# The GELU of the state space outputs: one ScalarE function, or square, tanh and two fused VectorE products

## The chip, the cores and the metric

The kernel runs on one core of one Trainium2 chip. The metric is the device time of one execution in microseconds (us), the median of several runs. Each run is one launch of the whole program.

## The reference, cut to what matters

The reference is one layer of a streaming encoder over 2048 prompt frames and 32 sample frames. After a norm and one input projection, half of the columns go through banded attention (`q`, `k`, `v`), the other half (`u`, 32 groups of 16 channels) through a diagonal state space scan. The scan's outputs are passed through a tanh-form GELU and a sigmoid gate; both halves are normed, joined and projected; a gated feed-forward block follows.

```python
ssm_y, h_last = _s5(u, h0, ...)
g = jax.nn.gelu(ssm_y)
ssm_o = g * jax.nn.sigmoid(g @ lw['ssm_glu_w'] + lw['ssm_glu_b'])
merged = concatenate([_rmsnorm(attn, ...), _rmsnorm(ssm_o, ...)])
x = x + g1 * (merged @ lw['w_out'])
```

`jax.nn.gelu` is here 0.5 y (1 + tanh(sqrt(2/pi) (y + 0.044715 y^3))).

## The kernel before, in words

Products of f32 quality are made of three matmuls each (`mm3`, L119; the matmul itself is L117): both operands are split into a rounded part and a rest (`split`, L112: ScalarE copies, VectorE or GpSimd subtracts).

The program has three stages that overlap at their edges. In the first (to about 380 us) come the input norm and the projections. In the second (about 380 to 592 us) three flows run beside each other: the 32 state space groups (`ssm_group`, L950 on, flow `fm`), the projections of six late tiles (`deferred`, flow `fd`) and the attention tiles (`attention_tile`, flow `fa`). Towards its end, the weights of the gate and of the output projection are split as well (`glu_steps`, `wo_steps`). In the third stage, from about 590 us, the gate (`c_prep`), the output projection (`c_out`) and the last attention tiles run, and then the feed-forward block, which takes the longer part of the time.

One state space group: the inputs are transposed into the PSUM tile `up`; `uh` and `ul` are split from it; six matmuls give `v1` and `v2` in PSUM; VectorE multiplies them by tables into `w` and `t`; GpSimd adds; two VectorE scans run over `w`; VectorE or GpSimd multiplies by the tables again; seven matmuls sum up the PSUM tile `y` (128 x 262); ScalarE writes GELU(y) into `g2`, which is the buffer of `t` again (L992). In the next step the SP queue sends `g2` to DRAM (`gt_d`, L994) and GpSimd copies four columns of it (`gsm`, L995). The third stage reads `gt_d` and `gsm` back.

`y` has one PSUM buffer (`YB` is 1), so the matmuls of the next group wait until `y` has been read. The SBUF tiles of a group (`part`) have five buffers (`PSB`), and up to seven groups are under way (`Flow(ssm_start, G, 7, 1)`). The steps of the flows are emitted by fixed counts (`FM`, `FDS`, `FAS`); the order on each engine is then set when the program is built, by a scheduler that goes by this emission and a simulated timeline (`schedule_with_timeline_sim=True`). Each engine takes its instructions in that order.

ScalarE functions in use: copies and squares everywhere, `Exp` in `softmax` (L1057, L1059), `Tanh` for the gate (L1326) and once at the start (L223), the GELU function (L992), and `Silu` in the feed-forward block (L1741). The program names no tables; the build puts an ACT_TABLE_LOAD where the next function is not in the loaded set.

Helpers: `act` (L100, its instructions on L101) is every ScalarE operation, `stt` (L97, L98) VectorE's fused `(a op0 scalar) op1 b`, `tt` (L88, L89) every two-operand operation on VectorE or GpSimd.

Of the kernel before, what the change touches and what calls it, by code (L numbers as in the profile page):

```python
# [10 lines left out]
F32 = mybir.dt.float32  # L11
F32R = mybir.dt.float32r
I32 = mybir.dt.int32
AF = mybir.ActivationFunctionType
ALU = mybir.AluOpType
AX = mybir.AxisListType
MULT, ADD, SUB = ALU.mult, ALU.add, ALU.subtract
# [56 lines left out]
def hybrid_kernel(  # L74
# [13 lines left out]
    def tt(e, out, a, b, op):  # L88
        e.tensor_tensor(out, a, b, op=op)  # L89
# [7 lines left out]
    def stt(out, a, s, b, op0, op1):  # L97
        V.scalar_tensor_tensor(out, a, s, b, op0=op0, op1=op1)  # L98

    def act(out, a, func=AF.Copy, **kw):  # L100
        A.activation(out, a, func, **kw)  # L101

    def f(a):
        return a.bitcast(F32)
# [7 lines left out]
    def split(hi, lo, src, eh, el):  # L112
        cp(eh, hi, src)
        tt(el, lo, src, f(hi), SUB)

    def mm(out, lhsT, rhs, start, stop, more=False):
        PE.matmul(out, lhsT, rhs, start=start, stop=stop, skip_group_check=more)  # L117

    def mm3(out, ah, al, bh, bl, start, stop, more=False):  # L119

        mm(out, ah, bh, start, False, more)
        mm(out, ah, bl, False, stop and al is None, more)
        if al is not None:
            mm(out, al, bh, False, stop, more)
# [797 lines left out]
    def mbank(shape, dt=F32, nm="mb", tag="mb", bufs=MB):  # L922
        return bs1.tile(shape, dt, tag=tag, name=nm, bufs=bufs)
# [23 lines left out]
    def part(t, dt=F32R):  # L947
        return pss.tile([128, XC], dt, tag=t, name=t)

    def ssm_group(g):  # L950
        b_, gi_ = divmod(g, GB)
        us, uss = bt_[b_]
        sm = pss.tile([128, SM], F32R, tag="sm", name="sm", bufs=SMB)
        SP.dma_start(f(sm), sm_d[g])
        ec = pss.tile([128, 2, XC], F32, tag="ec", name="ec", bufs=SMB)
        for h in range(2):
            SP.dma_start(ec[64 * h:64 * h + 64], e_d[g])
        Th, Tl = sm[:, 0:128], sm[:, 128:256]
        M1, M2 = f(sm[:, 256:384]), f(sm[:, 384:512])
        up = mbank([128, XC], nm="up")  # L960
        yield 1
        for b in range(2):
            PE.transpose(up[:, 128 * b:128 * b + 128], us[:, b, gi_].rearrange("c l h -> c (l h)"), ident)
        PE.transpose(up[:, 256:262], uss[:, gi_].rearrange("c l h -> c (l h)"), ident[0:6, 0:6])
        uh, ul = part("uh"), part("ul")
        split(uh, ul, up, A, V)
        yield 1
        v1 = mbank([128, XC], nm="v1", tag="v1", bufs=1)
        v2 = mbank([128, XC], nm="v2", tag="v2", bufs=1)
        mm3(v1, sm[:, 512:640], sm[:, 704:832], uh, ul, True, True)  # L970
        mm3(v2, sm[:, 576:704], sm[:, 768:896], uh, ul, True, True)
        w = part("w", F32)
        t = part("t", F32)
        tt(V, w[:, 1:XC], v1[:, 0:XC - 1], ec[:, 0, 1:XC], MULT)
        tt(V, t[:, 1:XC], v2[:, 0:XC - 1], ec[:, 1, 1:XC], MULT)
        tt(P, w[:, 1:XC], w[:, 1:XC], t[:, 1:XC], ADD)
        P.tensor_copy(w[:, 0:258:257], zh[:, g])
        V.tensor_tensor_scan(w[:, 1:257], r8[:, g:g + 1].to_broadcast([128, 256]), w[:, 1:257], 0.0, op0=MULT, op1=ADD)
        V.tensor_tensor_scan(w[:, 258:262], r8[:, g:g + 1].to_broadcast([128, 4]), w[:, 258:262],
                             zh[:, g, 1:2], op0=MULT, op1=ADD)  # L980
        yield 1
        for i, (e, xf) in enumerate(((P, xf1), (P if g % 2 else V, xf2))):
            x = w if i else t
            tt(e, x, w, ec[:, i], MULT)
            P.tensor_copy(xf[:, :, g], x[:, 256:262:5])
        yield 1
        y = mbank([128, XC], nm="y", tag="y", bufs=YB)
        mm3(y, Th, Tl, uh, ul, True, False)
        mm(y, M1, t, False, False)
        mm(y, M2, w, False, True)  # L990
        g2 = t
        act(g2, y, AF.Gelu_apprx_tanh)  # L992
        yield 1
        SP.dma_start(gt_d[16 * g:16 * g + 16].rearrange("h l c -> l h c"), g2[:, 0:256])  # L994
        P.tensor_copy(gsm[:, :, g], g2[:, 257:261])  # L995
        yield 1
# [3 lines left out]
    def ssm_start(g):  # L1000
        if g % GB == 2 and g // GB < 3:
            ssm_batch(g // GB + 1)
        return ssm_group(g)
# [905 lines left out]
```

## Time and profile before

| | us |
|---|---|
| median of 3 runs | 2326.4 (2324.03 to 2329.42) |
| the profiled execution | 2332.55 |
| its span, first to last instruction | 2330.8 |
| TensorE busy, of the span | 2211.3 |
| VectorE busy | 1718.3 |
| ScalarE busy | 1261.2 |
| GpSimd busy | 1256.3 |

The rows of the trace come from the profiled execution, which took 6.15 us more than the median; 1.75 us of its time lie outside the span. PE is TensorE, PEld its weight loads, DVE VectorE, ACT ScalarE, POOL GpSimd, SP the queue that issues the DMAs. A granted clock of 1.00 is 2.4 GHz, of 0.50 it is 1.2 GHz; values between are a mixture over a stretch.

### The profile page before, as it was taken

To read this page: it belongs to the slowest core of one execution; us is meant where nothing else is said; L and a number is where in the kernel's file an instruction comes from. 1 tells how busy PE (TensorE), PEld (TensorE's weight loads), DVE (VectorE), ACT (ScalarE), POOL (GpSimd) and SP (SyncE) were. 2 spreads that over 40 slices of the span, in tenths; PEclk is the share of its full clock that TensorE was granted. 3 is DMA by queue.
4 is the path that set the end of the run, shared out by engine and by line. 5 is a ranking of instruction groups with operands and counts; after the bars stand their busy time and mean duration, and the time that the engine had idled before them with its cause. 6 is when DMAs were issued, how large, how long until landed. Compare 5 with 4: busy or idle time off the path is not lost.

```text
span 2330.8 us, 39040 instructions
## 1 busy us (share of the span) xinstructions
PE 2211.3 (95%) x13286; PEld 2055.1 (88%) x13286; DVE 1718.3 (74%) x2737; ACT 1261.2 (54%) x2544; POOL 1256.3 (54%) x1173
## 2 busy tenths in 40 slices
PE   7888898898899999999999998999999999999999
PEld 4576776786788888799999998999999989999998
DVE  6888874678777884766768779556677796677887
ACT  6655443555666655544445566444455754444664
POOL 1167775776366764578884136555521375565122
PEclk8899998898899999999999999999999999999999
DMA  7757676676323125457666644643365436534653
GB/s 232 264 169 239 192 219 205 196 232 200 102 75 93 55 69 174 150 174 219 209 200 213 184 142 154 180 122 111 101 199 170 132 110 183 147 97 120 199 164 125
DMA packets 429573, 380.12 MB, mean 163 GB/s; under 512 B 57327, under 2 KB 358987, under 8 KB 429373
## 3 DMA queue, kind: packets, MB, share of 16 engines
q1 hardware_dynamic: 429372, 377.63, 53.1%
q8 instruction: 104, 1.70, 0.3%
q14 instruction: 97, 0.79, 0.1%
HBM read 284.63 MB, written 92.91 MB: 162 GB/s over the span
## 4 chain that ended last, share of the span: by engine, by line
PE 63%; DVE 6%; ACT 2%; issue 2%; POOL 1%; DMA 1%; SPq 0%; DVEq 0%; POOLq 0%; ACTq 0%
PE fx L117 30%; PE fy L117 15%; PE fz L117 8%; PE co L117 5%; PE cb L117 1%; PE ob L117 1%; DVE wl L89 1%; PE pt L1070 1%; PE ft L1454 1%; ACT pbuf L101 1%; DVE ss L1332 1%; DVE bl L89 0%; PE fo L1721 0%; PE s L117 0%; DVE gl L89 0%
## 5 line engine op out<-in xcount | busy, mean ns | idle before, releaser
L89 DVE TENSOR_TENSOR wl<-wr,wh 128x512 fp32r<-128x512 f32 (+1 forms) x708 | 641.0, 921 | 252.2 <-ACT wh L101 248.9
L101 ACT ACTIVATE wh<-wr 128x512 fp32r<-128x512 f32 (+1 forms) x708 | 431.1, 617 | 552.7 <-PE fx L117 301.5
L117 PE MATMUL fx<-bh,wh 128*128 128x352 f32 (+1 forms) x1576 | 507.4, 322 | 6.2 <-DVE acc L98 3.8
L117 PE MATMUL fx<-bl,wh 128*128 128x352 f32 (+1 forms) x1576 | 506.4, 321 | 4.3 <-DVE bl L89 4.3
L117 PE MATMUL fx<-bh,wl 128*128 128x352 f32 (+1 forms) x1576 | 507.4, 322 | 0.0
L89 POOL TENSOR_TENSOR wr<-wr 128x512 f32<-128x512 f32 x256 | 388.0, 1525 | 185.6 <-DVE wl L89 138.9
L117 PEld LDWEIGHTS fx<-bh,wh 128*128 128x128 f32 x1576 | 298.1, 189 | 6.9 <-DVE acc L98 4.0
L117 PEld LDWEIGHTS fx<-bl,wh 128*128 128x128 f32 x1576 | 298.0, 189 | 5.2 <-DVE bl L89 5.2
L117 PEld LDWEIGHTS fx<-bh,wl 128*128 128x128 f32 x1576 | 297.6, 189 | 0.1
L89 POOL TENSOR_TENSOR c<-c,acc 128x352 f32<-128x352 f32 (+1 forms) x72 | 93.0, 1296 | 311.0 <-ACT c L101 293.2
L117 PE MATMUL fy<-bh,wh 128*128 128x352 f32 (+1 forms) x792 | 254.8, 322 | 1.1 <-DVE acc L98 0.8
L117 PE MATMUL fy<-bh,wl 128*128 128x352 f32 (+1 forms) x792 | 254.1, 321 | 0.0
L117 PE MATMUL fy<-bl,wh 128*128 128x352 f32 (+1 forms) x792 | 253.7, 320 | 0.0
L89 POOL TENSOR_TENSOR c<-c 128x352 f32<-128x352 f32 (+1 forms) x96 | 135.8, 1416 | 174.5 <-ACT wh L101 73.6
L117 PEld LDWEIGHTS fy<-bh,wh 128*128 128x128 f32 x792 | 149.6, 189 | 1.6 <-DVE acc L98 1.0
L117 PEld LDWEIGHTS fy<-bl,wh 128*128 128x128 f32 x792 | 149.4, 189 | 0.0
L117 PEld LDWEIGHTS fy<-bh,wl 128*128 128x128 f32 x792 | 149.0, 188 | 0.0
L89 DVE TENSOR_TENSOR bl<-q,bh 128x1408 fp32r<-128x1408 f32 (+3 forms) x85 | 140.7, 1660 | 5.1 <-ACT bh L101 5.1
L117 PE MATMUL fz<-bh,wl 128*128 128x352 f32 (+1 forms) x412 | 132.2, 324 | 4.5 <-DVE wl L89 4.5
L117 PE MATMUL fz<-bh,wh 128*128 128x352 f32 (+1 forms) x412 | 133.6, 325 | 1.0 <-ACT wh L101 0.9
L117 PE MATMUL fz<-bl,wh 128*128 128x352 f32 (+1 forms) x412 | 132.6, 322 | 0.0
L101 ACT ACTIVATE bh<-q 128x1408 fp32r<-128x1408 f32 (+3 forms) x85 | 108.5, 1284 | 17.4 <-DVE q L89 14.6
(388 smaller groups left out, 5135.3 us busy)
## 6 DMA issues: line engine op xcount, KB each, us to landing
wr<-in_w_gate_dram SPq DMA_DIRECT2D x132, 256.0 KB
wr<-in_w_up_dram SPq DMA_DIRECT2D x132, 256.0 KB
wr<-sd_d SPq DMA_DIRECT2D x96, 256.0 KB
wr<-in_w_down_dram SPq DMA_DIRECT2D x72, 256.0 KB
adw<-in_w_ada_dram SPq DMA_DIRECT2D x64, 256.0 KB
f_d<-c SPq DMA_DIRECT2D x88, 176.0 KB
sm<-sm_d SPq DMA_DIRECT2D x32, 448.0 KB
q<-f_d SPq DMA_DIRECT2D x16, 704.0 KB
```

What stands on the lines that cost most here:

```text
L89: e.tensor_tensor(out, a, b, op=op)
L101: A.activation(out, a, func, **kw)
L117: PE.matmul(out, lhsT, rhs, start=start, stop=stop, skip_group_check=more)
L1070: PE.transpose(pt[:, kb, i * 128:(i + 1) * 128], pbuf[:, kv * npair + i, kb * 128:kb * 128 + 128], ident)
L1332: V.tensor_reduce(ss[:, 0:n], sq[:, :, 0:n].rearrange("p k n -> p n k"), AX.X, ADD)
L1454: PE.transpose(pb[:, 128 * i:128 * i + m], x[0:m, k * 128:(k + 1) * 128], ident[0:m, 0:m])
```

## The change: what it does

In `ssm_group` the one ScalarE instruction per group gives way to three on ScalarE (half of y, the square of y, a tanh) and two fused products on VectorE. `yh` reuses the buffer of `w`; `y2` is a new SBUF tile with five buffers. The result is written to the same `g2`.

```diff
         mm(y, M1, t, False, False)
         mm(y, M2, w, False, True)
         g2 = t
-        act(g2, y, AF.Gelu_apprx_tanh)
+        yh, y2 = w, part("y2", F32)
+        act(yh, y, scale=0.5)
+        act(y2, y, AF.Square)
+        stt(y2, y2, 1.0 / 0.044715, yh, ADD, MULT)
+        act(y2, y2, AF.Tanh, scale=2.0 * 0.044715 * math.sqrt(2.0 / math.pi))
+        stt(g2, y2, 1.0, yh, ADD, MULT)
         yield 1
         SP.dma_start(gt_d[16 * g:16 * g + 16].rearrange("h l c -> l h c"), g2[:, 0:256])
         P.tensor_copy(gsm[:, :, g], g2[:, 257:261])
```

## Rows read from the trace of the kernel before

**Rows 1.** The page, busy us and share of the span by engine.
```profile
PE 2211.3 (95%) x13286; PEld 2055.1 (88%) x13286; DVE 1718.3 (74%) x2737; ACT 1261.2 (54%) x2544; POOL 1256.3 (54%) x1173
```

**Rows 2.** Busy by stretch: length, PE, PEld, DVE, ACT, POOL, clock, DMA share, GB/s.
```profile
400.00:560.00 160.00, 143.96 (x902) 126.33 (x901) 112.77 (x255) 87.20 (x205) 115.98 (x216) 0.94 0.66 203
...
430.00:450.00 20.00, 15.88 (x87) 13.84 (x87) 10.94 (x31) 13.44 (x33) 11.90 (x25) 0.83 0.51 163
500.00:520.00 20.00, 20.00 (x143) 18.23 (x142) 17.94 (x37) 9.88 (x22) 18.85 (x38) 1.00 0.67 205
550.00:580.00 30.00, 22.12 (x118) 18.34 (x117) 29.19 (x57) 17.31 (x39) 23.90 (x43) 0.77 0.68 229
580.00:590.00 10.00, 5.96 (x40) 4.77 (x40) 4.08 (x10) 8.43 (x20) 2.48 (x4) 0.98 0.15 31
```

**Rows 3.** ScalarE groups, 380 to 592 us: busy us, mean ns, idle before them.
```profile
L101 ACT ACT_TABLE_LOAD x23 | 29.5, 1283 | 16.0 <-DVE st L89 11.2 <-issue 3.0 <-PE y L117 1.4
L101 ACT ACTIVATE t<-y 128x262 f32<-128x262 f32 x32 | 12.4, 388 | 9.5 <-PE y L117 6.1 <-issue 1.4 <-POOL t L89 0.9
```

**Rows 4.** TensorE in order of time, instructions after an idle time that ScalarE ended.
```profile
435.12 0.66 PE L1070 MATMUL pt<-cpk,pbuf 128*128 128x128 f32 x4 [3.08 <-ACT pbuf L101]
436.82 0.58 PE L117 MATMUL y<-uh,sm 128*128 128x262 f32 x1 [1.04 <-ACT t L101]
...
574.02 0.58 PE L117 MATMUL y<-uh,sm 128*128 128x262 f32 x1 [3.59 <-ACT t L101]
...
583.71 0.50 PE L117 MATMUL ob<-th,vs 128*128 128x256 f32 x2 [1.92 <-ACT pbuf L101]
...
586.56 0.33 PE L1234 MATMUL gsp<-cpk,gsm 128*128 128x128 f32 x1 [0.73 <-POOL gsm L995]
```

**Rows 5.** ScalarE in order of time, table loads ahead of those idle times.
```profile
432.86 1.28 ACT L101 ACT_TABLE_LOAD   x1 [7.42 <-DVE st L89]
...
435.09 1.28 ACT L101 ACT_TABLE_LOAD   x1
...
572.29 1.28 ACT L101 ACT_TABLE_LOAD   x1
...
581.45 1.28 ACT L101 ACT_TABLE_LOAD   x1
...
584.57 1.28 ACT L101 ACT_TABLE_LOAD   x1
585.86 0.39 ACT L101 ACTIVATE t<-y 128x262 f32<-128x262 f32 x1
```

**Rows 6.** ScalarE in order of time near 601 us: start, duration, operation.
```profile
601.39 1.28 ACT L101 ACT_TABLE_LOAD   x1 [1.30 <-DVE st L89]
...
604.28 0.48 ACT L101 ACTIVATE z<-cb,vecs 128x256 f32<-128x256 f32 x1
604.64 0.22 ACT L101 ACTIVATE st<-st 128x4 f32<-128x4 f32 x1
```

**Rows 7.** Waits from 380 to 592 us: us in total, times, longest.
```profile
POOL gsm L995 <- ACT t L101: 25.1, 13, 5.9
...
PE y L117 <- ACT t L101: 9.7, 7, 3.6
```

**Rows 8.** VectorE groups: busy us, mean ns, idle before.
```profile
L89 DVE TENSOR_TENSOR w<-w,ec 128x262 f32<-128x262 f32 x16 | 8.1, 505 | 1.3 <-POOL t L89 1.2
...
L98 DVE SCALAR_TENSOR_TENSOR z<-z,gr 128x256 f32<-128x256 f32 x32 | 30.7, 959 | 12.2 <-ACT z L101 12.1
```

**Rows 9.** Tile `w`: ns min/median/max, first and last start.
```profile
L89 POOL TENSOR_TENSOR w<-w,t x32: 729/747/1054, 390.6 to 563.9; 128x261 f32<-128x261 f32 x32
...
L89 DVE TENSOR_TENSOR w<-w,ec x16: 399/428/1341, 397.4 to 569.1; 128x262 f32<-128x262 f32 x16
```

**Rows 10.** Instructions that touch `y`, two stretches: PE, PEld, ACT (count).
```profile
500.00:520.00 20.00, 6.45 (x30) 4.57 (x30) 1.59 (x5) 1.00 0.67 205
550.00:580.00 30.00, 12.67 (x42) 7.94 (x41) 2.13 (x6) 0.77 0.68 229
```

## The prediction

> **What bounds the kernel now.** I read the busy shares first: TensorE is busy for 95% of the span [rows 1], so a change elsewhere counts only through the time in which TensorE stands or goes at the lower clock. Next the stretches around the 32 state space groups. From 400 to 560 us TensorE is busy for 143.96 of 160 us at a mean clock of 0.94, VectorE for 112.77, GpSimd for 115.98, ScalarE for 87.20 [rows 2]. No engine is full all the time; the reader should see that ScalarE, which the change relieves of table loads, is the emptiest of the four, and that VectorE, which gets new work, is at 17.94 of 20 us from 500 to 520 us and at 29.19 of 30 from 550 to 580 us [rows 2]. Then the groups of ScalarE: 23 table loads of 1.283 us, 29.5 us, against 12.4 us for all 32 GELUs [rows 3]. Last, the idle times of TensorE that ScalarE ended [rows 4], and what ScalarE did just ahead of them [rows 5]. What follows 592 us is carried along: a delay at the end of this stage moves the gate, the output projection and the feed-forward block by as much.
>
> **The table loads go.** Softmax needs the exponential, the GELU its own set, and the flows alternate, so ScalarE loads on the way there and back. At 601.39 us ScalarE loads for a softmax; the gate's tanh (`z`) and softmax's last exponential (`st`) then follow each other with no load between [rows 6], so tanh and the exponential share a set. With the GELU written in square, copy and tanh, the 23 loads of the stage and the one at 601.39 us have no cause left: 24 x 1.283 = 30.8 us of ScalarE. What of it TensorE feels is read stall by stall, as the smaller of the idle time and the load that stands in its chain. Of 3.08 us before 435.12 the load at 432.86 is 1.28; the 1.04 us before 436.82 are shorter than the load at 435.09; of 3.59 us before 574.02 the load is 1.28, the rest being weight copies ahead of it; of 1.92 before 583.71 it is 1.28; the 0.73 us before 586.56 end with a GpSimd copy that waited for the last GELU, itself behind two loads [rows 4, 5]. Sum: 1.28 + 1.04 + 1.28 + 1.28 + 0.73 = 5.61, **5.6 us gained**; I leave out the shorter stalls. Bounds: nothing, if another input comes just as late; and the five stalls in full, 10.4 us.
>
> The Trainium skill (ScalarE: Activation LUTs, "What ACT_TABLE_LOAD costs") counts a drain of about 1.38 us to each load, 2.66 us a switch. In this trace the GELU starts 0.01 us after the load at 584.57 has ended [rows 5], and no such drain stands behind the load; by the page the same five stalls would give 2.66 + 1.04 + 2.66 + 1.92 + 0.73 = 9.0 us and the sum would end 3.4 us lower. I go by the row.
>
> **Three ScalarE instructions for one.** A GELU takes 0.388 us [rows 3]; I price a half, a square and a tanh of the same shape alike, 64 more instructions, 24.8 us. As 30.8 us of loads go, ScalarE gets no fuller, and it was busy for only 87.20 of 160 us; the work itself costs nothing while that cover lasts. But `y` has one PSUM buffer, and it is now read twice before the next group may write it. TensorE waited for that reading 7 times [rows 7]; 7 x 0.39 = **2.7 us lost**. Bounds: nothing, and 32 x 0.39 = 12.5 us if every group waited. A second read cannot free the buffer earlier, so there is no gain below nothing.
>
> **Two VectorE products.** The trace has no such product of this shape. The nearest row by shape, engine and stage is the product of `w` with a table, both in SBUF: 0.505 us [rows 8]. The nearest by opcode is the gate's fused product of 256 columns, 0.959 us, with one strided operand [rows 8]; the lowest single product of `w` took 0.399 [rows 9]. I take 0.505, the row of the same stage and layout, and keep 0.399 and 0.959. 64 products are 32.3 us; VectorE has 47 us free between 400 and 560 [rows 2], so most of them fit. They do not fit where it is full. Five GELUs lie in 500 to 520 us and six in 550 to 580 [rows 10]: 17.94 + 10 x 0.505 = 22.99, 3.0 us over; 29.19 + 12 x 0.505 = 35.25, 5.25 us over. In the first stretch TensorE has no idle time at all [rows 2], so I count the 3.0 in full. Behind the second VectorE is busy for only 4.08 of 10 us [rows 2], and part of its full stretch is weight splitting that nothing waits for yet; I count half, 2.6. Together **5.6 us lost**; bounds nothing and 18.2 us (at 0.959: 22 x 0.959 less the 2.87 us that are free in the two stretches).
>
> **The new waits.** Tanh waits for VectorE, the second product for ScalarE. Behind the tanh stand copies of other groups and the exponentials, behind the product the subtractions and scans of other groups. The result comes later by a square, a product, a tanh and a product: 0.39 + 0.505 + 0.39 + 0.505, some 1.8 us. Who waits for it: GpSimd's `gsm` copy, which waited 13 times, 25.1 us in all [rows 7], and the SP queue's `gt_d` transfer with the loads behind it. Within the stage I cost this at nothing: GpSimd has 44 us free from 400 to 560 [rows 2] and the group loads run several groups ahead. If that cover is gone, GpSimd's products for later groups are late, and the scans behind them. For the last group, which holds up the gate, the 1.8 us replace two loads, 2.57 us [rows 5], so its share is the 0.73 already counted. The new tile adds no DMA, and `w` is held to the end of the GELU, as `t` was before. The order of the instructions may shift a little everywhere in this stage; that is of unknown sign and lies in the range.
>
> **The sum.** -5.6 + 2.7 + 5.6 = +2.7 us. The profiled execution took 2332.55, so 2335.25; it stood 6.15 above the median, so 2329.1 us. A change of 0.2%, 4.7 us, is about what a measurement of this kernel can tell from none; the forecast is no change, with a lean to slower.
>
> **Rivals.**
> - *The loads were worth more (faster).* If the products run in VectorE's waiting times, nothing is lost there, and shorter stalls keep the clock up: from 430 to 450 us, with two of the five stalls in it, the granted clock was 0.83, and 15.88 us of TensorE work at full clock would take 15.88 x 0.17 = 2.7 us less [rows 2]. -5.6 + 2.7 - 2.7 = -5.6 us, 2320.8; with the stalls in full -10.4 + 2.7 - 2.7, 2316.0. For it: VectorE's 47 us. Against it: the two full stretches.
> - *VectorE and GpSimd block each other (slower).* Both operands of the new products lie in SBUF. Operations of that kind vary while GpSimd works: the product of `w` took from 0.399 to 1.341 us, and GpSimd's own sum from 0.729 to 1.054 [rows 9]. At the middle of the two rows, 0.732 us, 22 products are 16.1 us, 13.2 over, none absorbed: -5.6 + 2.7 + 13.2 = +10.3, 2336.7; at 0.959 it is 2341.7. It decides as soon as the products take over about 0.5 us and their backlog all reaches the gate. For it: GpSimd is busy for 18.85 of 20 us in the first full stretch [rows 2]. Against it: the median of 0.428 [rows 9]. The Trainium skill (SBUF — State Buffer, "SBUF: two separate sides") states such a rule: a VectorE operation with two SBUF inputs and a GpSimd operation that reads SBUF shut each other out for a whole instruction. The spread of these rows agrees; by the rule at its worst each product waits out a GpSimd sum, 0.399 + 0.747 = 1.15 us, and the time would be 2346.
> - *The loads stay.* If the build put tanh into another set than the exponential, nothing is gained: +8.3 us, 2334.7. The rows after 601 us speak against it [rows 6].
>
> **How the numbers follow.** Forecast 0.38, its own range 2323 (the products at nothing) to 2334 (their 8.2 us over in full and half the gain from the loads); faster rival 0.30; slower rival 0.29; loads stay 0.03. Faster by over 0.2% (below 2321.7): 0.26 of the first rival and 0.02 of the forecast, 0.28. Slower (above 2331.1): 0.27 + 0.07 + 0.02 = 0.36. The rest, 0.36, is within. From 2315 to 2340 the range takes in the faster rival down to its full stalls and the slower one nearly to its upper price; some 0.14 is left out at the two ends.
>
> **What would show it.** Right: no table loads from 380 to 602 us; ScalarE idle ahead of the tanhs; VectorE products of about 0.5 us; TensorE's waits before 436.8 and 574.0 shorter, new ones behind VectorE near 500 to 520 and 550 to 580; the stage ending within some 5 us of 592. Wrong: products near 0.4 with VectorE's idle time shrunk by as much (faster), products near 0.8 or GpSimd late by several us with the clock down (slower), or a stage of the same length and a difference elsewhere.

## The result and the profile after

The changed kernel takes 2342.41 us (median of 3 runs, 2339.47 to 2342.69) against 2326.4. The ratio on record is 1.005, interval 1.0031 to 1.0068, so 7 to 16 us slower. (The quotient of these two medians, of 3 runs each, is 1.0069, just above the interval; against the 2330 us that later runs gave for the kernel before, it is 1.0053.) The ratio is within the forecast's range (1.005 of 2326.4 is 2338.0 us), the median 2.4 us above its upper end. The forecast was no change with a lean to slower, and gave no change and slower 0.36 each; the lean was right, the size was not.

The page of the changed kernel, span and busy time by engine, answers to [rows 1]:

```profile
span 2340.9 us, 39168 instructions
...
PE 2209.9 (94%) x13286; PEld 2051.7 (88%) x13286; DVE 1752.5 (75%) x2801; ACT 1249.9 (53%) x2584; POOL 1266.7 (54%) x1173
```

The span grew by 10.1 us, TensorE's busy time by nothing. VectorE has 64 instructions and 34 us more, ScalarE 40 instructions more (64 new ones, 24 loads fewer) and 11 us less.

The groups of ScalarE answer to [rows 3]; the first line is of the whole span, the two below of 380 to 592 us. The trace leaves the number of `y2` out and names `yh` by its buffer, `w`.

```profile
L101 ACT ACT_TABLE_LOAD x2 | 2.6, 1283 | 2.8 <-DMA csl<-in_c_sample_dram 2.8
...
L101 ACT ACTIVATE y<-y 128x262 f32<-128x262 f32 x64 | 25.9, 407 | 39.4 <-DVE y L98 39.3
...
L101 ACT ACTIVATE w<-y 128x262 f32<-128x262 f32 x32 | 12.5, 389 | 5.4 <-PE y L117 4.6 <-POOL tabg L89 0.5 <-POOL gsm L1000 0.2
```

All 24 loads between 380 and 602 us are gone. In their place stand 96 instructions of 38.4 us and one new idle time: ScalarE stood 39.3 us for the first product, ahead of a tanh.

VectorE's groups from 380 to 592 us, answering to [rows 8]:

```profile
L98 DVE SCALAR_TENSOR_TENSOR y<-y,w 128x262 f32<-128x262 f32 x32 | 19.0, 594 | 0.5 <-ACT y L101 0.5
...
L98 DVE SCALAR_TENSOR_TENSOR t<-y,w 128x262 f32<-128x262 f32 x32 | 17.2, 536 | 0.5 <-ACT y L101 0.4
...
L89 DVE TENSOR_TENSOR w<-w,ec 128x262 f32<-128x262 f32 x16 | 11.1, 693 | 0.5 <-POOL t L89 0.5
```

The products took 0.594 and 0.536 us in the mean, 36.2 us in all, and the old product of `w` beside them grew from 0.505 to 0.693 us. VectorE itself hardly ever waits for ScalarE (0.5 and 0.4 us in all ahead of the two kinds of product): a product stands behind VectorE's other work, not behind its input.

The stretches of [rows 2] after the change: length, PE, PEld, DVE, ACT, POOL, clock, DMA share, GB/s.

```profile
400.00:560.00 160.00, 142.46 (x879) 122.06 (x878) 139.44 (x311) 77.44 (x232) 129.88 (x226) 0.96 0.70 215
500.00:520.00 20.00, 18.04 (x113) 15.66 (x113) 15.67 (x38) 8.66 (x29) 18.93 (x32) 0.91 0.65 205
550.00:580.00 30.00, 17.77 (x100) 14.16 (x99) 28.18 (x55) 20.18 (x55) 15.75 (x30) 0.83 0.56 194
580.00:590.00 10.00, 7.69 (x34) 6.76 (x33) 5.79 (x15) 6.02 (x21) 3.05 (x3) 0.50 0.69 135
```

VectorE went from 112.77 to 139.44 of 160 us; its 47 us of free time are now 21.

**Where the 10 us are.** I cut the span at two events: the first matmul of the output projection (`co`) and the first of the feed-forward block (`fx`). Same columns as above; before first:

```profile
380.00:594.60 214.60, 184.27 (x1098) 159.48 (x1098) 151.49 (x330) 122.02 (x280) 146.36 (x265) 0.89 0.64 199
594.60:950.50 355.90, 345.35 (x2124) 300.66 (x2123) 256.14 (x440) 211.13 (x557) 211.36 (x195) 0.98 0.32 98
```

and after:

```profile
380.00:589.20 209.20, 177.99 (x1053) 151.33 (x1052) 175.79 (x385) 107.54 (x311) 153.54 (x262) 0.91 0.65 201
589.20:959.40 370.20, 351.85 (x2156) 306.84 (x2154) 263.10 (x448) 212.38 (x564) 215.07 (x197) 0.97 0.30 94
```

The second stage, the one that was changed, became 5.4 us shorter. The third, in which no line was changed, became 14.3 us longer. Read the counts of PE: 45 matmuls fewer between 380 us and `co`, 32 more behind it; the other 13 had run before 380 us. Counted in the trace, 2586 matmuls stood ahead of the first `co`, and now 2554 do. The 32 that moved are attention's: 12 of tile `ob` (96 ahead of `co` instead of 108), 8 of `qb` (40 instead of 48), 8 of `pt` and 4 of `kb`. The instructions of tile `ob` in the second stage, before and after:

```profile
380.00:594.60 214.60, 17.95 (x108) 15.59 (x108) 3.42 (x8) 2.98 (x8) 0.89 0.64 199
...
380.00:589.20 209.20, 17.21 (x96) 14.78 (x96) 2.99 (x7) 2.60 (x7) 0.91 0.65 201
```

As TensorE takes its instructions in the order that the build set, these counts are fixed in the program; they do not come from how long anything took in this execution. What attention did not get done beside the state space groups it does in the third stage, where TensorE was already busy for 97% of the time. There TensorE's busy time rose by 6.5 us and its idle time by 7.8 (10.55 to 18.35).

### The profile page after: what moved, and what is told of

Its sections match the earlier page's. It is cut to its first block, busy times and chain, and to the rows that moved or that the text cites. A ratio compares the mean times of both kernels' runs of the same rounds, so it can differ in the third digit from the quotient of the medians.

```text
span 2340.9 us, 39168 instructions
## 1 busy us (share of the span) xinstructions
PE 2209.9 (94%) x13286; PEld 2051.7 (88%) x13286; DVE 1752.5 (75%) x2801; ACT 1249.9 (53%) x2584; POOL 1266.7 (54%) x1173
## 4 chain that ended last, share of the span: by engine, by line
PE 57%; DVE 8%; POOL 3%; issue 3%; ACT 2%; DMA 2%; SPq 0%; DVEq 0%; POOLq 0%; ACTq 0%
PE fx L117 29%; PE fy L117 15%; PE fz L117 8%; PE co L117 3%; DVE wl L89 1%; PE cb L117 1%; DMA wr<-in_w_up_dram 1%; ACT pbuf L101 1%; PE ob L117 1%; POOL xc L89 1%; DVE gl L89 1%; POOL pbuf L89 1%; DVE tl L89 1%; DVE bl L89 1%; PE pt L1075 1%
## 5 line engine op out<-in xcount | busy, mean ns | idle before, releaser
L101 ACT ACTIVATE bh<-q 128x1408 fp32r<-128x1408 f32 (+3 forms) x85 | 108.5, 1283 | 16.6 <-DVE q L89 13.8
```

## The experiments

Intervals are of the ratio to the kernel before, run on the same chip; its medians there were 2329.8 to 2332.0 us. Us beside a ratio are the ratio's distance from 1 times 2330.

### The loads alone

```diff
-        act(g2, y, AF.Gelu_apprx_tanh)
+        act(g2, y, AF.Tanh)
```

> The GELU function is replaced by a bare tanh, so the activation is another function and its outputs are not the reference's; the instructions and their order on every engine are those of the kernel before, without 24 table loads. All theories: this is the gain of the loads alone. By the sum of the prediction -5.6 us (ratio 0.9976), not under -10.4 (0.9955). If the loads were always covered by something else, 0 (1.000).

Measured: 0.993 (0.9916 to 0.9944), 2314.29 us: 16.3 us gained (13.0 to 19.6), three times the 5.6 of the forecast and above its upper bound of 10.4. This is the cleanest of the runs: TensorE, VectorE, GpSimd and SP have the same instructions in the same order as before, and ScalarE lacks the 24 loads and nothing else. The two stretches:

```profile
380.00:577.00 197.00, 176.30 (x1097) 153.06 (x1096) 150.52 (x329) 92.29 (x257) 147.63 (x265) 0.93 0.70 214
577.00:932.90 355.90, 345.73 (x2123) 301.22 (x2123) 257.06 (x441) 210.38 (x556) 211.47 (x195) 0.98 0.32 98
```

The third stage is the same to a tenth of a us. In the second, TensorE's idle time fell by 9.6 us (30.3 to 20.7), and its busy time by 8.0 with the same matmuls. Busy time times granted clock is 164.0 us in both (184.27 x 0.89, 176.30 x 0.93): the clock accounts for the 8.0 us.

The waits of TensorE from 380 to 600 us say which idle time it was. Before (with the 9.7 us of `y` in [rows 7]):

```profile
PE pt L1070 <- ACT pbuf L101: 5.0, 3, 3.1
...
PE ob L117 <- ACT pbuf L101: 1.9, 1, 1.9
```

With the loads gone:

```profile
PE y L117 <- ACT t L101: 4.4, 4, 2.1
PE pt L1070 <- ACT pbuf L101: 2.8, 2, 1.8
...
PE ob L117 <- ACT pbuf L101: 0.5, 1, 0.5
```

In these three, 16.6 us of waiting for ScalarE became 7.7. How it builds up is seen on ScalarE in order of time. Before, the GELU and the softmax exponential (`st`) behind it each have a load ahead of them:

```profile
401.69 1.28 ACT L101 ACT_TABLE_LOAD   x1
402.98 0.39 ACT L101 ACTIVATE t<-y 128x262 f32<-128x262 f32 x1
403.39 1.28 ACT L101 ACT_TABLE_LOAD   x1
404.68 0.20 ACT L101 ACTIVATE st<-st 128x4 f32<-128x4 f32 x1
...
436.38 0.39 ACT L101 ACTIVATE t<-y 128x262 f32<-128x262 f32 x1
```

With the loads gone:

```profile
400.82 0.39 ACT L101 ACTIVATE t<-y 128x262 f32<-128x262 f32 x1
401.11 0.20 ACT L101 ACTIVATE st<-st 128x4 f32<-128x4 f32 x1
...
430.18 0.39 ACT L101 ACTIVATE t<-y 128x262 f32<-128x262 f32 x1
...
568.36 0.40 ACT L101 ACTIVATE t<-y 128x262 f32<-128x262 f32 x1
```

The function of `y` is 2.2 us earlier at the first shown, 6.2 at the one that stood at 436.38 us, and 17.5 at the last, which stood at 585.86 [rows 5]. Of 30.8 us of loads more than half came through, although ScalarE has idle time: here it is idle behind the points at which others waited for it, and a load ahead of such a point delays all of them.

### The products alone

```diff
         act(g2, y, AF.Gelu_apprx_tanh)
+        stt(g2, g2, 1.0, w, MULT, ADD)
+        stt(g2, g2, 1.0, w, MULT, SUB)
```

> The GELU function and its table loads stay; two fused products of the same shape on VectorE follow it (each multiplies and adds with w, so the outputs are not the reference's). Theory V (the 64 products crowd VectorE and push attention work into the third stage): as slow as the changed kernel or slower, ratio 1.005 to 1.009, with fewer attention matmuls done when the third stage starts. Theory S (the loss comes from the longer chain on ScalarE and the y bank read twice): within 0.1% of before. Theory O (any new order of the build costs or gains some us by chance): anything from 0.996 to 1.006.

In fact these two add `w` and take it away again, so nothing of the computation is left out. Measured: 1.0054 (1.0039 to 1.007), 12.6 us slower (9 to 16), about the loss of the change itself, with all the loads still there. The products took 0.580 us each. Before `co` 96 `ob` and 40 `qb` matmuls were done, and the third stage took 363.8 us. That VectorE's products cost more than the 5.6 us of the forecast follows, for the order that the build took here; whether two products without a round trip cost as much in the changed kernel is a question for the runs below.

### The change without its products

```diff
-        stt(y2, y2, 1.0 / 0.044715, yh, ADD, MULT)
-        act(y2, y2, AF.Tanh, scale=2.0 * 0.044715 * math.sqrt(2.0 / math.pi))
-        stt(g2, y2, 1.0, yh, ADD, MULT)
+        act(g2, y2, AF.Tanh, scale=2.0 * 0.044715 * math.sqrt(2.0 / math.pi))
```

> Half, square and tanh on ScalarE as in the change, without the two products on VectorE (the result is the tanh of the scaled square, not the GELU). Theory V: faster than before, 0.997 to 0.999, the gain of the loads less a second read of y. Theory S: as slow as the changed kernel, 1.003 to 1.006. Theory O: anything from 0.996 to 1.006.

Measured: 0.9923 (0.9905 to 0.9941), 2313.11 us, as fast as the run with the loads alone, and faster than either theory of the expectation said. Two things follow. Reading `y` twice and the two further ScalarE instructions cost nothing that can be seen. And all the loss of the change is in the products and what they make others wait for: from here to the changed kernel it is 1.005 less 0.9923, 29.6 us. Both stages:

```profile
380.00:574.80 194.80, 176.45 (x1100) 155.20 (x1099) 148.84 (x331) 112.27 (x322) 147.05 (x265) 0.92 0.71 220
574.80:930.10 355.30, 341.35 (x2125) 297.35 (x2123) 260.68 (x439) 208.77 (x554) 212.28 (x195) 0.98 0.32 97
```

108 `ob` and 48 `qb` matmuls are done before `co`, as before the change, and the third stage has its old length. This is the kernel to hold the change against. In the second stage TensorE stands idle for 18.4 us here and for 31.2 in the changed kernel. That stage is 14.4 us longer in the changed kernel (209.2 against 194.8), and the third 14.9 (370.2 against 355.3). So the products, with the waits that they bring, cost about as much in the stage that they stand in as behind it; the 5.4 us by which the changed stage beats the kernel before are 19.8 won without the loads, less those 14.4.

### One product, two products, and the round trip

One product (the second only; a different function of `y` again):

```diff
-        stt(y2, y2, 1.0 / 0.044715, yh, ADD, MULT)
         act(y2, y2, AF.Tanh, scale=2.0 * 0.044715 * math.sqrt(2.0 / math.pi))
         stt(g2, y2, 1.0, yh, ADD, MULT)
```

> Half, square and tanh on ScalarE and one product on VectorE behind the tanh (the first product is left out, so the result is not the GELU). Between no product (0.9923) and two products behind the tanh (1.0017). Theory C (each product costs about the same): 0.995 to 0.999. If only the second product overfills VectorE: 0.992 to 0.995; if any product brings the order that defers attention: 0.999 to 1.003.

Measured: 0.9982 (0.997 to 0.9994).

Both products behind the tanh, so that ScalarE waits for no product:

```diff
-        stt(y2, y2, 1.0 / 0.044715, yh, ADD, MULT)
         act(y2, y2, AF.Tanh, scale=2.0 * 0.044715 * math.sqrt(2.0 / math.pi))
+        stt(y2, y2, 1.0 / 0.044715, yh, ADD, MULT)
         stt(g2, y2, 1.0, yh, ADD, MULT)
```

> The same instructions as the changed kernel, with the first product moved behind the tanh, so ScalarE does half, square and tanh without waiting for VectorE (the tanh is that of the bare square, so the outputs are not the reference's). Theory C (the time of the 64 products on VectorE is what costs): no better than the changed kernel, 1.003 to 1.007. Theory R (the wait of the tanh for VectorE costs, since it holds up all that stands behind it on ScalarE): 0.996 to 1.000, some 12 us or more given back.

Measured: 1.0017 (1.0007 to 1.0028), between what the two theories expected. The series is 0.9923 with no product, 0.9982 with one, 1.0017 with two, 1.005 with two and the tanh between them. In us, from step to step: 13.7, 8.2 and 7.7, each uncertain by 4 to 5. So some 22 us go with VectorE's work as such and 7.7 with the waiting between the engines, if the order of the instructions is the same throughout; the next runs show how far it isn't. The second stage of the one-product run, and both stages of the two-product run (these from an execution of 2340.52 us, 7.4 above that run's median):

```profile
380.00:573.90 193.90, 172.74 (x1072) 149.40 (x1070) 161.94 (x357) 110.56 (x315) 151.33 (x264) 0.93 0.70 219
...
380.00:590.30 210.30, 179.72 (x1066) 154.69 (x1065) 177.61 (x387) 111.13 (x313) 153.67 (x263) 0.90 0.65 201
590.30:957.70 367.40, 350.49 (x2156) 305.16 (x2155) 265.21 (x447) 213.72 (x564) 215.84 (x197) 0.97 0.31 95
```

With two, VectorE is busy for 177.61 of 210.3 us, and the third stage is 12.1 us longer than with no products; one product already makes it 369.5. The attention matmuls move with the first product (96 `ob` before `co`), the second stage grows with the second (193.9 to 210.3), and TensorE's idle time in it with that (21.2 to 30.6; 31.2 with the tanh between).

### What the order alone is worth

The build sets the order on every engine anew for each kernel. To price that, the same work with odd and even groups swapped between VectorE and GpSimd (in the change, too):

```diff
-        for i, (e, xf) in enumerate(((P, xf1), (P if g % 2 else V, xf2))):
+        for i, (e, xf) in enumerate(((P, xf1), (V if g % 2 else P, xf2))):
```

> The kernel before with the same work: only which groups (odd or even) take their second table product on VectorE and which on GpSimd is swapped, so the build finds another order. Theories V and S: within 0.1% of before. Theory O: the time moves by 0.2% or more, up or down.

Measured, on the kernel before: 1.0023 (1.0013 to 1.0034), 5.4 us for no change of work.

> The changed kernel with odd and even groups swapped in which engine takes the second table product: the same work, another order of the build. If the loss belongs to the change (work and waits of the products), 1.002 to 1.008 against the kernel before; if it was the luck of one order, it can as well be 0.997 or 1.000.

Measured, on the changed kernel: 1.0099 (1.0084 to 1.0115), 2353.68 us. The loss against before thus does not hang on the one order; against its own parity twin (1.0023) it is 0.0076, against before 0.005. But two orders of the same work lie 0.2 to 0.5% apart (5.4 and 11.4 us), and the 7.7 us of the round trip are no more than that, nor is the step of 8.2. The first of these runs also shows how an order can win a stage and lose the kernel:

```profile
380.00:578.00 198.00, 172.28 (x1076) 150.49 (x1075) 140.16 (x319) 111.68 (x266) 145.97 (x264) 0.92 0.68 209
578.00:951.10 373.10, 353.68 (x2149) 306.03 (x2148) 271.52 (x451) 215.58 (x567) 211.44 (x196) 0.96 0.32 98
```

The second stage is 16.6 us shorter than before, the third 17.2 longer, with 96 `ob` matmuls done ahead of `co` in place of 108: the same exchange as in the change. No work was added to VectorE here, so attention can be deferred by the order alone. In the swapped change it is 84 `ob` matmuls, and the third stage takes 387.1 us.

### Taking other work off VectorE

If the loss is VectorE's fullness, moving other work off it should bring it back. Three attention copies go to ScalarE, which the change relieved:

```diff
-            cp(V if x else A, out[64 * x:64 * x + 64], obv[64 * x:64 * x + 64, :, x])
+            cp(A, out[64 * x:64 * x + 64], obv[64 * x:64 * x + 64, :, x])
...
-            cp(V if hb else A, qtv[:, hb * 4:hb * 4 + 4], f(qb[:, :, 0:n]).rearrange("p h (o q) -> p h o q", q=qw))
+            cp(A, qtv[:, hb * 4:hb * 4 + 4], f(qb[:, :, 0:n]).rearrange("p h (o q) -> p h o q", q=qw))
...
-                V.tensor_copy(kt[:, :, 0:128], f(vprev[1][:, :, 128:256]))
+                act(kt[:, :, 0:128], f(vprev[1][:, :, 128:256]))
```

> The changed kernel with three of attention's copies (half of qt, half of att, the old half of kt) moved from VectorE to ScalarE; some 14 us of VectorE's time from 380 to 592 us go to ScalarE, which the loads left free, and more in the third stage. Theory C: much of the products' cost comes back, 0.994 to 1.000. Theory R: the tanh still waits, 1.002 to 1.006.

Measured: 0.9978 (0.9967 to 0.9988); 0.0072, 16.8 us, better than the change. The second stage takes 204.3 us against 209.2, the third 360.2 against 370.2, so two thirds of the gain lie in the third stage, where there are no products. The third stage:

```profile
584.30:944.50 360.20, 350.50 (x2170) 306.27 (x2171) 241.71 (x406) 237.29 (x620) 216.41 (x198) 0.98 0.32 98
```

VectorE is busy for 241.71 us in it instead of 263.10, and TensorE idle for 9.7 instead of 18.35, although more of attention is deferred (84 `ob` matmuls ahead of `co` instead of 96). So the number of deferred matmuls alone does not set the price: with 96 ahead of `co`, the runs of this document have third stages from 358.3 to 373.1 us. The control, the same three lines in the kernel before:

> The kernel before with the same three copies moved to ScalarE, GELU function and loads kept: the control for e7. Theory C: little changes, 0.997 to 1.003, as VectorE was not what held the stage up and ScalarE's loads were. Theory R: the same range.

Measured: 0.9991 (0.9982 to 1.0), 2.1 us, at the edge of what can be told from none. The copies are worth much in the kernel with the products and next to nothing in the one without. (The control's own order has 28 table loads; the control below has 22, the kernel before 26.) One step further, with the second table product always on GpSimd:

```diff
-        for i, (e, xf) in enumerate(((P, xf1), (P if g % 2 else V, xf2))):
+        for i, (e, xf) in enumerate(((P, xf1), (P, xf2))):
```

> As e7, and the second table product of every group on GpSimd (before: every other one), another 8 us off VectorE. Theory C: as e7 or up to 0.3% faster, unless GpSimd is then the full engine. Theory R: 1.002 to 1.006.

Measured: 0.996 (0.9948 to 0.9972), 2320.15 us. And its control, the same lines with the GELU function and its loads kept:

> The kernel before with the three copies on ScalarE and the second table product always on GpSimd, GELU function and loads kept: the control for the best run. If that run's 0.996 comes from the written-out GELU on a VectorE that has been relieved, this one is 0.998 to 1.002, above it; if the moves themselves are the gain, it is 0.996 or below.

Measured: 0.9943 (0.9928 to 0.9958), 2317.7 us, the fastest of the kernels that leave nothing out. With VectorE relieved, the GELU written out (0.996) is still not better than the function (0.9943); the two intervals overlap. From 400 to 560 us (the second from an execution of 2327.29 us, 9.6 above its median), the version with the GELU written out:

```profile
400.00:560.00 160.00, 143.22 (x928) 124.61 (x928) 141.06 (x300) 93.41 (x270) 143.00 (x249) 0.99 0.76 234
```

and the one with the function:

```profile
400.00:560.00 160.00, 146.52 (x931) 128.49 (x931) 106.88 (x243) 91.95 (x220) 129.68 (x246) 0.96 0.68 211
```

Written out, VectorE and GpSimd are both at 88% or more, VectorE no less than in the change itself (139.44 us); with the function VectorE has a third of its time free.

### Fewer loads without the products

The GELU function kept, but for four groups at a time, from a copy of `y`, so that the flows alternate less often:

```diff
-        g2 = t
-        act(g2, y, AF.Gelu_apprx_tanh)
-        yield 1
...
+        if g % 4 == 0:
+            yb_[0] = pss.tile([128, 4, XC], F32, tag="yb", name="yb", bufs=2)
+        yb = yb_[0]
+        cp(A, yb[:, g % 4], y)
+        if g % 4 == 3:
+            act(yb, yb, AF.Gelu_apprx_tanh)
+        yield 1
+        if g % 4 == 3:
...
```

> The GELU function kept, but taken for four groups at a time: y is copied into a tile of four groups, and every fourth group one GELU runs over 1048 columns; 12 of the 26 table loads go, VectorE gets nothing. If loads cost what the run with the bare tanh shows (some 16 us for 24), half of that comes back less the copies on ScalarE: 0.995 to 0.999. If the later results of three groups in four hold up GpSimd or the end of the stage: 1.000 to 1.004.

Measured: 1.0025 (1.0013 to 1.0037): a miss. 14 loads are left instead of 26 in the whole span, and the second stage is 12.4 us shorter than before:

```profile
380.00:582.20 202.20, 173.22 (x1069) 150.66 (x1068) 147.32 (x324) 113.21 (x270) 141.18 (x240) 0.92 0.70 209
582.20:954.10 371.90, 354.02 (x2145) 307.67 (x2145) 268.82 (x447) 214.24 (x563) 213.69 (x196) 0.96 0.31 94
```

The third stage is 16.0 us longer, with 96 `ob` matmuls before `co`. Once more attention is deferred and the stage before it shorter, so the 12.4 us are not the loads' alone. Whether the batches of four deferred attention, or the new order as such, this run does not show.

## Why the prediction was right or wrong

**The loads: the term was a third of its size.** The step that failed is "What of it TensorE feels is read stall by stall, as the smaller of the idle time and the load that stands in its chain", 5.6 us; the run with the loads alone gave 16.3. Two things were left out. The stalls were cut to one load each and the short ones dropped, but the loads add up on an engine that takes its work in order: TensorE's idle time fell by 9.6 us, and the three waits for ScalarE shown above by 8.9, near the bound of the five stalls in full, 10.4. And the clock stood only in the rival, at 2.7 us; over the whole stage it gave back 8.0. The rival "the loads were worth more" had the mechanism, and nothing else of it came true. The Trainium skill (ScalarE: Activation LUTs, "What ACT_TABLE_LOAD costs") counts 2.66 us a switch, from which the estimate here was 9.0 us, nearer but short too; the drain it counts was not seen in the rows (the load at 403.39 us starts 0.02 us after the GELU ends, and its exponential 0.01 us after it), and the sum of 16.3 does not need one.

**The second read of `y`: 2.7 us, nothing measured.** "TensorE waited for that reading 7 times" holds for before; after, it waits once, 1.9 us:

```profile
ACT y L101 <- DVE y L98: 39.3, 25, 3.5
...
POOL gsm L1000 <- DVE t L98: 11.1, 7, 4.3
...
PE y L117 <- ACT y L101: 1.9, 1, 1.9
```

Much of the 9.7 us of [rows 7] had been loads ahead of the reading, not the reading.

**The two products: 5.6 us, some 22 measured.** A duration of 0.505 us was a fair estimate (0.565 measured). What failed is "VectorE has 47 us free between 400 and 560, so most of them fit", and with it the sum over two full stretches. The same windows did not even get fuller (15.67 of 20 us, 28.18 of 30): the build spread the work otherwise. What the runs show in its place: the time rises with the products, the 29.6 us lie half in the second stage and half in the third, and work taken off VectorE brings 16.8 back. That the products took from attention, which shares VectorE, what it needed to keep up is an argument: with one product it is deferred, but it is so too where only the order was changed. The upper bound of 18.2 us was too low for the same reason: it was summed over 22 products in two stretches, not over 64.

**The new waits, costed at nothing.** TensorE's idle time in the second stage is 31.2 us after against 30.3 before, which looks as if "the group loads run several groups ahead" had been cover enough. But the stalls of the loads are in the 30.3. Without loads it is 20.7, without loads and products 18.4, so the change brought 10.5 to 12.8 us of new idle time, nearly all of which was there with two products and no round trip (30.6, in the execution 7.4 us above its median). The largest single wait stands at the end of the stage. In order of time across the engines, at the last groups:

```profile
573.12 0.39 ACT L101 ACTIVATE y<-y 128x262 f32<-128x262 f32 x1
...
575.72 0.74 DVE L98 SCALAR_TENSOR_TENSOR wol<-wf,vecs,woh 128x512 fp32r<-128x512 f32 x1
...
577.50 0.42 DVE L98 SCALAR_TENSOR_TENSOR y<-y,w 128x262 f32<-128x262 f32 x1
...
577.96 0.42 ACT L101 ACTIVATE y<-y 128x262 f32<-128x262 f32 x1 [3.50 <-DVE y L98]
...
578.48 0.43 DVE L98 SCALAR_TENSOR_TENSOR t<-y,w 128x262 f32<-128x262 f32 x1
...
578.97 0.19 POOL L1000 COPY gsm<-t 128x4 f32<-128x4 f32 x1 [0.46 <-DVE t L98]
...
579.22 0.47 PE L1239 MATMUL gsp<-cpk,gsm 128*128 128x128 f32 x1 [5.15 <-POOL gsm L1000]
```

The square is done at 573.5 us; its product runs at 577.5, behind weight splitting (`wol`) and the row maxima of softmax. The tanh waits 3.50 us, and TensorE 5.15 for what follows, where "its share is the 0.73 already counted" stood. Over all groups the round trip is the last step of the series, 7.7 us, no more than what an order can do. The shift of the order itself, which the prediction left "of unknown sign" in its range, was worth 5.4 and 11.4 us in the two runs that swapped the groups.

**The sum.** -17.9 us (loads gone, `y` read twice), +21.9 (products), +7.7 (round trip) add up to +11.7, as they must, since the runs are steps of one series. The forecast of +2.7 was the small difference of two terms that were both too small by more than 10 us. The two errors, 15.0 and 24.0 us, have opposite signs and leave 9.0 between them; that the ratio still fell into the range is luck.

**The rivals.** That the loads stay is excluded: the two loads left are elsewhere. In "VectorE and GpSimd block each other" the mechanism is in the trace, at a lower price: 0.732 us a product was not reached in the mean (0.565). Its sum, +10.3 us, is near the +11.7 measured, but it comes from 22 products in two full stretches, and the loss measured runs through both stages. The products, tile `w` after, ns min/median/max:

```profile
L98 DVE SCALAR_TENSOR_TENSOR y<-y,w x32: 399/432/1176, 401.4 to 577.5; 128x262 f32<-128x262 f32 x32
...
L98 DVE SCALAR_TENSOR_TENSOR t<-y,w x32: 355/420/1308, 402.7 to 578.5; 128x262 f32<-128x262 f32 x32
```

At their medians the 64 would take 27.3 us instead of 36.2, so 8.9 us of VectorE time lie in the long ones. Of the 64, 19 took over 0.6 us. Each of these 19 started while GpSimd was in an operation on two tiles, and each ended 0.28 to 0.29 us after that operation did. The longest:

```profile
417.63 1.29 POOL L89 TENSOR_TENSOR qs<-qkv,qs 128x512 fp32r<-128x512 f32 x1 [0.47 <-ACT qs L101]
...
417.90 1.31 DVE L98 SCALAR_TENSOR_TENSOR t<-y,w 128x262 f32<-128x262 f32 x1
```

The rule of the Trainium skill (SBUF — State Buffer, "SBUF: two separate sides") that a VectorE operation with two SBUF inputs and a GpSimd operation that reads SBUF shut each other out agrees with these 19. It does not show in every pair: an operation of ten columns on GpSimd (`ms`, 128 x 10) held up none of the five products that started under it, which took 0.40 to 0.42 us. No run took GpSimd's operations away, so what the blocking cost the kernel was not measured; with one product, hence less of it, the attention matmuls had moved already.

**What stays open.** Whether the 7.7 us are the round trip or another order: no run has both in the same order. How the third stage's 14.3 us divide between attention's deferred matmuls (busy time +6.5 us) and waits that its new order brings (idle time +7.8 us), and why the same number of deferred matmuls goes with third stages 15 us apart. No run added the products in the order of before, so the 22 us hold for the orders that the build chose.

## What to carry to other kernels

To price a stall source on an in-order engine, put in an instruction of the same shape that lacks it: with the orders unchanged, one run gave 16.3 us where summing stalls had given 5.6, the clock included. Free time of a shared engine is no room for new work until you have asked which flow loses its turn and where that flow's work ends up; read the stage behind, not only the stage that was changed. And before believing half a per cent, run the same work in another order: here that alone moved the time by 0.2 to 0.5%.

## What the runs showed of the hardware that was not expected

24 table loads of 1.283 us, 30.8 us on an engine busy for 57% of the stage (122.02 of 214.6 us), held up the whole kernel by 16.3 us. Half of that, 8.0 us, was TensorE running the same matmuls at a granted clock of 0.89 instead of 0.93: at the two levels of 1.2 and 2.4 GHz, 22% of the stage at the lower one against 14%. A VectorE product of one shape, both inputs in SBUF, took from 0.355 to 1.308 us in one kernel, and all 19 of 64 that took over 0.6 us ended 0.28 to 0.29 us after a GpSimd operation that was running when they started.
